# Two more gates in the stage of sums, keys at the opening of the memory heads, four begun products

## The chip, the cores and the metric

One core of a Trainium2 chip runs the whole kernel. The metric is the device time of one execution in microseconds (us), the median over runs.

The engines are PE (matmul; PEld is its weight load), DVE (vector), ACT (scalar), POOL (GpSimd) and SP, whose queue issues nearly all DMAs. Matmuls accumulate in banks of 128 x 512 float32 (PSUM), which ACT and DVE empty.

## What is computed

A two-layer encoder on 1024 tokens of width 1024, all in float32. The change lies in layer 2 (`l % 2 == 1`), in its front and its end:

```
h = rmsnorm(x, norm_gain[l])
mk, mv = jnp.split(memn @ w_mem_kv[l], 2, axis=-1)       # 256 memory tokens, 4 heads of 128
qc, kc, vc, qm, gate = split_cols(h @ w_in_odd[o], SPLIT_ODD)   # 1024, 1024, 1024, 512, 1536 columns
yc = neighborhood_attn(qc, kc, vc, rpb_c[o])             # 16 heads of 64 on a 16 x 64 grid, 8 x 16 windows
ym = memory_attn(qm, mk, mv)                             # 4 heads
y = jnp.concatenate([yc, ym], axis=-1) * jax.nn.silu(gate)
x = x + y @ w_out_odd[o]
return rmsnorm(x, final_norm_gain)
```

## The kernel before, in words

Every matmul operand of full precision is kept as two rounded parts, a high one and a low one (`wh`/`wl` for weights, `H` for the normalised tokens, `k`, `q`, `v`, `ph`/`pl` elsewhere); a product is the sum hi·hi + hi·lo + lo·hi, three matmuls for each 128 rows of the contraction. Columns of the projection come in tiles of 128: `O_Q` (8 tiles of queries), `O_K` (8 of keys, two heads each), `O_V` (8 of values), `O_QM` (4 memory queries), `O_G` (12 gates). A projected tile of 128 columns by 1024 tokens takes 48 matmuls of 512 columns.

Layer 2 has three stages.

*The stage of sums* (`front`, L1617). Pairs of column tiles are multiplied by seven products of half size instead of eight (sums and differences of token halves t1 to t4, of weight parts, and of results), 84 matmuls of 512 for a pair. `pairs` lists the pairs: eight gates (0 to 3 and 8 to 11), the memory queries and the queries; the tuple after it gives the order of the results' use, and `PLAN` says between which products the values of heads 0 to 3 are computed. Results go to HBM (`gd`, `mqd`, `qd`).

*The heads* (`odd`). First the eight half memory heads: `scores(n)` and the product with the memory values. Then the near heads (`near`), 16 heads over 136 steps, each with scores (`s`), the softmax (L1114 on DVE with its bias `bm`, L1117 on ACT or L1118/L1119 on DVE and POOL), a transpose of the result `pn` on PE (`tr`), the split into `ph` (ACT, L125) and `pl` (DVE, L542), and the product with the values (`pv`). A head's keys and values must be there when it starts. What layer 2 still has to project is the generator `work()`: its products are called *filler* and are put between the steps of the heads in a fixed ration of columns: 16 x 1536 columns ahead of the first score, `SLOT` columns at each of 32 places of the memory heads, `STEP` columns at each near step. In work() stand gate 4, the values of heads 4 to 7 (`of_two`, four blocks of 48 matmuls of 256 columns; a block fills one bank, and is then copied out by ACT L125 and DVE L425 in two halves), the keys (`keys(j)`, two halves of eight steps, 24 matmuls each; after the second half the high and low parts `k` are doubled to the other 64 partitions by DMAs, L366 and L367), gates 5, 6 and 7, and at last `begin_out`: the first two products of the output projection, which need the y rows 0 to 5 as operands (`first`, loaded at L1231 into tiles k, q and v, already in two parts). `todo` is the order of the later part; a task's weights are loaded while the one ahead of it runs.

PSUM has two banks each of the tags "s", "tr", "pv" and "pj". All filler goes through the two "pj" banks in turn.

*The output projection* (`out_project`, L1332 for products of y, L1345 for products of the sums t1 to t4 of y). It is again done by seven products. It takes the banks that `begin_out` has filled (`begun`), then adds its own. The sums t1 to t4 are split into high and low parts by ACT L125 and DVE L129, and results are added into `H`, `mk`, `sg`, `yb` tiles by DVE L1357.

PE runs its matmuls in the order of the program. The other engines' orders are set when the kernel is built, by a scheduler that weighs the instructions with offsets (`AHEAD`); each engine then runs its list in order, and so does SP's queue of DMAs.

## Time and profile before

| | |
|---|---|
| time, median of 3 runs | 1487.73 us (1485.93 to 1492.74) |
| profiled execution | span 1486.8 us; its own device time is not listed apart from the three runs, 1485.93, 1487.73 and 1492.74 us |
| PE busy | 1467.6 us, 99% |
| DVE, ACT, POOL busy | 1030.7, 837.2, 644.2 us |
| granted TensorE clock | 0.998 on average |
| memory heads | about 1030 to 1122 us |
| near heads | about 1123 to 1364 us |
| output projection | from 1364 us |

The profile's rows by time have the start, the length, the engine, the line, and out<-in by the names of the tiles; what stands in brackets is the idle time ahead and what ended it. A row of a chain is start, length and what ran or was waited for. A row of a table of windows has the window, its length, and for each engine its busy time with the number of instructions. A row of waits says who waited for whom: total, times, longest.

### The profile page before, as it was taken

The numbers are of one execution on the slowest core, as the hardware profiler recorded it, in microseconds if no ns is written. First come the engines' busy times: TensorE is split into PE (matmuls) and PEld (weight loads), VectorE is DVE, ScalarE is ACT, GpSimd is POOL, SyncE is SP. The second block draws the span as 40 slices with busy tenths as digits, with TensorE's granted clock in tenths as the row PEclk, the third lists the DMA queues.
The fourth block names the chain that finished last, engine by engine and source line by source line (L and its number), as shares of the span: only waits on it lengthen the run. The fifth ranks groups of instructions, "written<-read, shape, count | busy, mean of one in ns | idle before, by whom it ended". The sixth has DMA issues, their size and how long they took to land.

```text
span 1486.8 us, 25511 instructions
## 1 busy us (share of the span) xinstructions
PE 1467.6 (99%) x8433; PEld 1274.7 (86%) x8433; DVE 1030.7 (69%) x2124; ACT 837.2 (56%) x1877; POOL 644.2 (43%) x767
## 2 busy tenths in 40 slices
PE   9999999999999999999999999999999999999998
PEld 8898898988888788888879987888998898888886
DVE  6687777677776577776687776664446787778674
ACT  7743665556655456654544444444446777777454
POOL 1223668556765746543450000001425556665454
PEclk9999999999999999999999999999999999999999
DMA  8966334434443424388553343567665568789834
GB/s 287 306 160 181 118 125 160 123 120 133 126 137 112 155 78 144 100 276 303 187 176 127 128 135 137 157 169 241 233 242 170 188 198 269 246 283 323 314 105 144
DMA packets 173860, 271.92 MB, mean 183 GB/s; under 512 B 15648, under 2 KB 96800, under 8 KB 172704
## 3 DMA queue, kind: packets, MB, share of 16 engines
q1 hardware_dynamic: 173296, 270.20, 56.4%
q8 instruction: 67, 1.10, 0.3%
q14 instruction: 65, 0.53, 0.1%
q10 hardware_dynamic: 432, 0.09, 0.0%
HBM read 174.28 MB, written 83.89 MB: 174 GB/s over the span
## 4 chain that ended last, share of the span: by engine, by line
PE 86%; DMA 6%; DVE 3%; ACT 2%; issue 1%; SPq 1%; POOL 1%; POOLq 0%; ACTq 0%; DVEq 0%
PE pj L242 16%; PE pj L62 11%; PE x L1617 6%; PE tr L133 6%; PE pv L1066 4%; PE y L1617 4%; PE pv L62 3%; PE s L62 3%; PE pj L1332 3%; PE tr L62 3%; PE sa L1332 2%; PE pv L1617 2%; PE sa L1033 2%; PE s L1332 2%; PE sa L1034 2%; PE pj L851 2%
## 5 line engine op out<-in xcount | busy, mean ns | idle before, releaser
L542 DVE TENSOR_TENSOR pl<-tr,ph 128x512 fp32r<-128x512 f32 (+2 forms) x352 | 203.9, 594 | 45.5 <-ACT ph L125 43.6
L125 ACT ACTIVATE ph<-tr 128x512 fp32r<-128x512 f32 (+2 forms) x352 | 176.2, 522 | 103.7 <-PE tr L133 79.7
L242 PE MATMUL pj<-H,wh 128*128 128x512 f32 x704 | 233.2, 411 | 0.6 <-DVE vt L313 0.2
L158 POOL TENSOR_SCALAR wh<-wraw 128x512 fp32r<-128x512 f32 x48 | 32.2, 673 | 275.2 <-PE x L1617 236.0
L125 ACT ACTIVATE wh<-wraw 128x384 fp32r<-128x384 f32 (+1 forms) x163 | 88.7, 553 | 99.6 <-PE pj L1332 12.2
L242 PE MATMUL pj<-H,wl 128*128 128x512 f32 x352 | 139.2, 395 | 0.0
L242 PEld LDWEIGHTS pj<-H,wh 128*128 128x128 f32 x704 | 120.6, 189 | 19.3 <-issue 0.6
L62 PE MATMUL pj<-H,wh 128*128 128x512 f32 x384 | 121.0, 396 | 0.0
L1119 POOL TENSOR_SCALAR pn<-pn,st 128x384 f32<-128x384 f32 (+1 forms) x128 | 72.7, 569 | 102.1 <-DVE st L1118 62.0
L133 PE MATMUL tr<-ident,P 128*128 128x128 f32 x752 | 115.4, 273 | 0.3 <-POOL P L719 0.2
L1279 POOL TENSOR_TENSOR wl<-wraw,wh 128x384 fp32r<-128x384 f32 x56 | 62.9, 1125 | 91.5 <-ACT wh L125 89.2
L1117 ACT ACTIVATE pn<-pn,st 128x384 f32<-128x384 f32 (+1 forms) x128 | 75.1, 587 | 41.8 <-DVE st L1114 40.5
L133 PEld LDWEIGHTS tr<-ident,P 128*128 128x128 f32 x752 | 88.9, 140 | 8.2 <-POOL P L719 1.2
L1039 ACT ACTIVATE P<-sa,st 128x1024 f32<-128x1024 f32 x64 | 71.4, 1117 | 35.3 <-PE tr L133 19.1
L1041 POOL TENSOR_SCALAR P<-P,st 128x1024 f32<-128x1024 f32 x64 | 74.6, 1169 | 27.9 <-DVE st L1040 27.3
L1038 DVE TENSOR_REDUCE st<-sa 128x1 f32<-128x1024 f32 x64 | 77.5, 1218 | 8.3 <-PE sa L1034 7.6
L62 PE MATMUL s<-k,q 128*128 128x384 f32 (+1 forms) x352 | 81.2, 327 | 0.0
L242 PEld LDWEIGHTS pj<-H,wl 128*128 128x128 f32 x352 | 66.2, 188 | 15.1
L62 PE MATMUL pj<-H,wl 128*128 128x512 f32 x192 | 75.6, 394 | 0.0
L160 POOL TENSOR_TENSOR wl<-wraw,wh 128x512 fp32r<-128x512 f32 x52 | 69.6, 1341 | 10.3 <-ACT wh L125 7.8
L851 PE MATMUL pj<-ah,H 128*128 128x256 f32 x384 | 70.8, 282 | 1.0 <-ACT ah L125 0.6
L62 PEld LDWEIGHTS pj<-H,wh 128*128 128x128 f32 x384 | 66.6, 188 | 5.4
(568 smaller groups left out, 4186.7 us busy)
## 6 DMA issues: line engine op xcount, KB each, us to landing
wraw<-w_o SPq DMA_DIRECT2D x52, 256.0 KB, 3.7
y<-yb SPq DMA_DIRECT2D x24, 512.0 KB, 3.4
wraw<-s SPq DMA_DIRECT2D x64, 192.0 KB, 3.9
wraw<-w_e SPq DMA_DIRECT2D x44, 256.0 KB, 3.3
k<-k SPq DMA_DIRECT2D x42, 256.0 KB, 5.9
s<-bias SPq DMA_DIRECT2D x56, 192.0 KB, 2.0
wq<-w_o SPq DMA_DIRECT2D x40, 256.0 KB, 3.3
y<-sg SPq DMA_DIRECT2D x18, 512.0 KB, 3.5
```

The lines of the kernel that those rows point to most:

```text
L62: return lambda *a, **k: self.tc.keep_in_program_order(getattr(self.engine, name)(*a, **k))
L125: return self.nc.scalar.activation(out, in_, AF.Copy, scale=scale)
L133: self.turned = self.fence = self.pe.transpose(o, i, self.ident)
L242: self.pe.matmul(a[:, :n], s[:, kt % UNIT, :], m, start=(kt == 0 and i == 0), stop=(kt == KT - 1 and i == 2))
L542: self.low = nc.vector.tensor_tensor(pl[:, :n], tr[:, :n], ph[:, :n], op=OP.subtract)
L851: self.last = nc.tensor.matmul(a[:, b * 256:(b + 1) * 256], x[kt][:, t], w, start=(kt + b + i == 0), stop=(kt == KT - 1 and i == 2), skip_ ...
L1038: nc.vector.tensor_reduce(st[:, 0:1], s, axis=AX.X, op=OP.max, negate=True)
L1041: self.normal = nc.gpsimd.tensor_scalar(pt, pt, st[:, 2:3], 0.5, op0=OP.mult, op1=OP.mult)
L1117: nc.scalar.activation(o, o, AF.Exp, bias=st[:, 0:1], scale=-1.0, accum_out=st[:, 2:3])
L1119: self.normal = normal = nc.gpsimd.tensor_scalar(o, o, st[:, 3:4], 0.5, op0=OP.mult, op1=OP.mult)
L1332: last = nc.tensor.matmul(bank, s[:, k, :], y[3 * u + k][m][:, cols], start=start and u + k + e == 0, stop=u == 1 and k + e == 4, skip_gro ...
L1617: self.last = nc.tensor.matmul(bank, ws[s][:, k, :], b[k][m], start=start and k + i == 0, stop=k == UNIT - 1 and i == 2, skip_group_check= ...
```

## The change

Gates 4 and 5 leave the filler and become an eleventh pair of the stage of sums, run fourth. With less filler the rations change: 3400 columns a slot in the memory heads instead of 4150, and in the near heads 1825 for steps 0 to 108, 1125 for steps 109 to 119 and 2304 for steps 120 to 135, instead of 1930 for all.

The heads open with keys 0 instead of gate 4; both pairs of values (heads 4, 5 and 6, 7) use the tag "v" in one piece; seven steps of keys 1 come ahead of the second pair of values. Gate 7 goes through in two halves, the second at the very end.

`begin_out` makes four products instead of two, the last two in the banks of the tag "s"; the output projection starts with all four begun.

```
--- before.py
+++ after.py
@@ -24,8 +24,8 @@
 NEG = -1e30
 UNIT = 4
 PLAN = "x.xx.V1V1V2V1V1V1V2V1V1V1V2V1V1V1V2V1x2z2V1V1V2V1V1V1V2V1V1V1V2V1V1V1V2V1z4z2z2"
-SLOT = 4150
-STEP = 1930
+SLOT = 3400
+STEP = ((109, 1825), (120, 1125), (136, 2304))
 
 
 E_QA, E_KA, E_VA, E_QB, E_KB, E_VB, E_QM, E_G = 0, 4, 5, 6, 10, 11, 12, 16
@@ -1294,7 +1294,7 @@
         ws = deque(parts(0, u) for u in range(2))
         yield 0
         for i in range(n):
-            p = self.ps("pj")
+            p = self.ps("pj" if i < 2 else "s")
             banks.append(p)
             for u in range(2):
                 h, l = ws.popleft()
@@ -1302,7 +1302,7 @@
                     for e, (s, m) in enumerate(((h, 0), (h, 1), (l, 0))):
                         self.pe.matmul(p, s[:, k, :], first[3 * u + k][m], start=u + k + e == 0,
                                        stop=u == 1 and k + e == 4, skip_group_check=True)
-                    if k == 0:
+                    if k == 0 and i < 3:
                         ws.append(parts(i + 1, u))
                     yield 1536
         self.early = ws
@@ -1860,7 +1860,7 @@
                     if nt >= O_G:
                         return "gate", gd[nt - O_G]
                     return ("mem", mqd[nt - O_QM]) if nt >= O_QM else ("q", qd[nt])
-                pairs = [(n, n + 1) for n in (O_G + 8, O_G + 10, O_G, O_G + 2, O_QM, O_QM + 2, O_Q, O_Q + 2, O_Q + 4, O_Q + 6)]
+                pairs = [(n, n + 1) for n in (O_G + 8, O_G + 10, O_G, O_G + 2, O_QM, O_QM + 2, O_Q, O_Q + 2, O_Q + 4, O_Q + 6, O_G + 4)]
                 def values():
                     a, b = (self.values_of_two(wo[O_V + 2 * i:O_V + 2 * i + 2], vd[i], t, ("y", "pv"), "vt", 4, nc.vector)
                             for i, t in enumerate(("t3", "t4")))
@@ -1872,7 +1872,7 @@
                     yield from a
                     yield from b
                 v2 = values()
-                self.front(wo, pairs, (0, 1, 2, 4, 5, 6, 7, 8, 9, 3), v2, PLAN, x1, rows1, dests)
+                self.front(wo, pairs, (0, 1, 2, 10, 4, 5, 6, 7, 8, 9, 3), v2, PLAN, x1, rows1, dests)
             self.pools = {}
             mid.close()
             self.alias = {"P": "k"}
@@ -1903,9 +1903,8 @@
                         nc.sync.dma_start(io["out"][2 * p:2 * p + 2, :, c0:c0 + n].rearrange("k p t -> p k t"), x)
 
                 self.offset = AHEAD["out1"]
-                x = begun + [self.ps("s") for _ in range(2)]
                 y = [self.ps(t) for t in ("tr", "tr", "pv", "pv")]
-                self.out_project(io["w_oo"], sd[1], yd[1], x1d, done, OUT[1], (x, y), first, 2, last=True)
+                self.out_project(io["w_oo"], sd[1], yd[1], x1d, done, OUT[1], (begun, y), first, 4, last=True)
 
     def even(self, w, ka, qa, va, mq, qd, kvd, yd, sd, sd2):
         nc = self.nc
@@ -2017,28 +2016,26 @@
         half = lambda k, c: (O_G + k, self.gate_out(w, O_G + k, gd[k], [(c, 512)]))
 
         def work():
-            a, b = of_two(4, "v", 1), of_two(6, "k", 2)
-            g = self.gate_out(w, O_G + 4, gd[4])
-            now = next(g)
+            a, b = of_two(4, "v", 1), of_two(6, "v", 1)
+            k = keys(0)
+            now = next(k)
             next(a)
             yield now
-            yield from g
+            yield from k
+            self.ready[O_K + 1] = self.units(w, O_K + 1)
+            yield from a
+            made["bm"] = [self.near_bias(i) for i in range(2)]
             next(b)
-            yield from a
-            self.ready[O_K] = self.units(w, O_K)
+            k = keys(1)
+            for _ in range(7):
+                yield next(k)
             yield from b
-            k = keys(0)
-            now = next(k)
-            self.ready[O_K + 1] = self.units(w, O_K + 1)
-            yield now
-            yield from k
-            made["bm"] = [self.near_bias(i) for i in range(2)]
             made["v0"] = load_v(0)
-            todo = [(O_K + 1, keys(1)), (O_K + 2, keys(2)), half(5, 0), (O_K + 3, keys(3)), half(5, 512), (O_K + 4, keys(4)),
-                    (O_K + 5, keys(5)), half(6, 0), (O_K + 6, keys(6)), half(6, 512), (O_K + 7, keys(7)),
-                    (O_G + 7, self.gate_out(w, O_G + 7, gd[7]))]
+            made["open"] = True
+            todo = [(O_K + 1, k), (O_K + 2, keys(2)), half(6, 0), (O_K + 3, keys(3)), half(6, 512), (O_K + 4, keys(4)),
+                    (O_K + 5, keys(5)), half(7, 0), (O_K + 6, keys(6)), (O_K + 7, keys(7)), half(7, 512)]
             coming = iter(())
-            begin = self.begin_out(self.io["w_oo"], first, begun, 2)
+            begin = self.begin_out(self.io["w_oo"], first, begun, 4)
             for i, (_, steps) in enumerate(todo):
                 deque(coming, 0)
                 now = next(steps)
@@ -2046,8 +2043,6 @@
                     coming = self.jobs_of(w, todo[i + 1][0])
                 yield now
                 for k, now in enumerate(steps):
-                    if i == 0 and k == 6:
-                        made["open"] = True
                     if i == len(todo) - 1 and k == 4:
                         next(begin)
                     yield now
@@ -2115,7 +2110,7 @@
         while "open" not in made:
             fill(1)
         self.due = 0
-        self.near(made, load_q, load_v, gate, yd, lambda n: fill(STEP))
+        self.near(made, load_q, load_v, gate, yd, lambda n: fill(next(c for end, c in STEP if n < end)))
         deque(todo, 0)
         self.pe = nc.tensor
         return first, begun
```

On PE the values of heads 6, 7 look like this before: the last three matmuls of a block (`pj_2407`, the last block of heads 4, 5) and the first of the next one (`pj_2423`). The two are in different banks.

```order
L62 MATMUL pj_2407_11996<-v_2341_11571,H_1846_8875 128x256
L62 MATMUL pj_2407_11996<-v_2342_11572,H_1846_8875 128x256
L62 MATMUL pj_2407_11996<-v_2341_11571,H_1854_8883 128x256
L62 MATMUL pj_2423_12117<-k_2353_11658,H_1839_8868 128x256
L62 MATMUL pj_2423_12117<-k_2355_11660,H_1839_8868 128x256
L62 MATMUL pj_2423_12117<-k_2353_11658,H_1847_8876 128x256
```

And with the change, the end of the first block of heads 6, 7 (`pj_2485`) and the beginning of the second (`pj_2507`), with products of a memory head between them; both blocks are in the same bank, since the other is held by the first half of keys 1.

```order
L62 MATMUL pj_2485_12411<-v_2465_12323,H_1846_8875 128x256
L62 MATMUL pj_2485_12411<-v_2466_12324,H_1846_8875 128x256
L62 MATMUL pj_2485_12411<-v_2465_12323,H_1854_8883 128x256
L62 MATMUL pv_2494_12496<-ph_2497_12507,k_2440_12175 128x256 x2
L62 MATMUL pv_2494_12496<-pl_2498_12508,k_2440_12175 128x256
L62 MATMUL pv_2494_12496<-ph_2499_12511,k_2440_12175 128x256 x2
L62 MATMUL pv_2494_12496<-pl_2500_12512,k_2440_12175 128x256
L62 MATMUL pj_2507_12549<-v_2465_12323,H_1839_8868 128x256
L62 MATMUL pj_2507_12549<-v_2466_12324,H_1839_8868 128x256
L62 MATMUL pj_2507_12549<-v_2465_12323,H_1847_8876 128x256
```

What moved: two blocks in a row, in turn in two banks before, now use one bank, with six matmuls of 256 columns between them.

Key 6, whose doubled parts are read first by the score that begins its first head. Before, the last matmul of its second half (`pj_3195`) is followed by these rows on PE, and the first score that reads it (`k_3180` high, `k_3181` low) comes 79 rows later:

```order
L62 MATMUL pj_3195_15081<-H_1846_8875,wl_3098_14752 128x512
L62 MATMUL s_3240_15253<-k_3032_14523,q_3064_14625 128x384
L62 MATMUL s_3240_15253<-k_3033_14524,q_3064_14625 128x384
L62 MATMUL pv_3238_15238<-ph_3217_15167,v_3113_14802 128x384
L62 MATMUL pv_3238_15238<-pl_3218_15168,v_3113_14802 128x384
L62 MATMUL pj_3243_15264<-H_1839_8868,wh_3145_14919 128x512
```

```order
L62 MATMUL tr_3300_15450<-ident_1_63,pn_3257_15298 128x128
L62 MATMUL tr_3300_15450<-ident_1_63,pn_3260_15313 128x128
L62 MATMUL tr_3300_15450<-ident_1_63,pn_3269_15345 128x128
L62 MATMUL s_3303_15458<-k_3180_15042,q_3193_15075 128x256
L62 MATMUL s_3303_15458<-k_3181_15043,q_3193_15075 128x256
```

With the change, the last matmul of key 6 is on `pj_3246`, its parts are `k_3237` and `k_3238`, and only 28 matmuls stand between:

```order
L62 MATMUL pj_3246_15270<-H_1846_8875,wl_3146_14923 128x512
L62 MATMUL tr_3287_15435<-ident_1_63,pn_3254_15293 128x128
L62 MATMUL tr_3287_15435<-ident_1_63,pn_3260_15313 128x128
L62 MATMUL tr_3290_15442<-ident_1_63,pn_3254_15293 128x128
L62 MATMUL tr_3290_15442<-ident_1_63,pn_3260_15313 128x128
L62 MATMUL tr_3290_15442<-ident_1_63,pn_3269_15345 128x128
L62 MATMUL s_3293_15450<-k_3081_14698,q_3078_14689 128x384
L62 MATMUL s_3293_15450<-k_3082_14699,q_3078_14689 128x384
L62 MATMUL pv_3258_15304<-ph_3275_15380,v_3125_14853 128x384
L62 MATMUL pv_3258_15304<-pl_3276_15381,v_3125_14853 128x384
```

```order
L62 MATMUL tr_3308_15496<-ident_1_63,pn_3272_15362 128x128
L62 MATMUL tr_3311_15504<-ident_1_63,pn_3269_15345 128x128
L62 MATMUL tr_3311_15504<-ident_1_63,pn_3272_15362 128x128
L62 MATMUL tr_3311_15504<-ident_1_63,pn_3281_15394 128x128
L62 MATMUL s_3314_15512<-k_3237_15245,q_3208_15135 128x256
L62 MATMUL s_3314_15512<-k_3238_15246,q_3208_15135 128x256
```

What moved: the key's end, by the smaller ration of filler, towards the head that uses it. All 28 are of near steps and of the filler that follows (`pj_3296`, keys 7).

The end of the near heads on DVE, where the last low parts of the near heads (L542), the sums (L1357) and the low parts of t1 (`k_3596` and on, L129) follow each other. Before:

```order
L542 TENSOR_TENSOR pl_3564_16385<-tr_3562_16380,ph_3563_16384 128x384
L542 TENSOR_TENSOR pl_3567_16392<-tr_3565_16388,ph_3566_16391 128x256
L1357 TENSOR_TENSOR H_3576_16431<-H_3576_16431,pj_3492_16135 128x512
L1357 TENSOR_TENSOR H_3576_16431<-H_3576_16431,pj_3528_16265 128x512
L129 TENSOR_TENSOR k_3596_16507<-k_3596_16507 128x512
L129 TENSOR_TENSOR k_3597_16508<-k_3597_16508 128x512
L129 TENSOR_TENSOR k_3598_16509<-k_3598_16509 128x512
```

With the change, where the low parts of t1 are `k_3605` and on:

```order
L542 TENSOR_TENSOR pl_3581_16438<-tr_3579_16433,ph_3580_16437 128x384
L542 TENSOR_TENSOR pl_3584_16445<-tr_3582_16441,ph_3583_16444 128x256
L1357 TENSOR_TENSOR H_3591_16494<-H_3591_16494,pj_3477_16081 128x512
L1357 TENSOR_TENSOR H_3591_16494<-H_3591_16494,pj_3520_16220 128x512
L1357 TENSOR_TENSOR H_3592_16495<-H_3592_16495,s_3553_16337 128x512
L129 TENSOR_TENSOR k_3605_16522<-k_3605_16522 128x512
L129 TENSOR_TENSOR k_3606_16523<-k_3606_16523 128x512
L129 TENSOR_TENSOR k_3607_16524<-k_3607_16524 128x512
```

What moved: a third sum (`s_3553`, the third begun product) and a fourth low part now stand in this row, and on PE the products of t1 follow the near heads at once, where before the two products on `s_3570` and `s_3571` (36 matmuls of 512) came first.

49 lines of the change are left out of this document (22 added, 27 removed).

## Prediction

> **What bounds the kernel now.** I read the page first, then a table of stages, then the list of waits of layer 2, and last the single places that the change touches. The head of the page and its row of granted clock:
>
> ```profile
> span 1486.8 us, 25511 instructions
> PE 1467.6 (99%) x8433; PEld 1274.7 (86%) x8433; DVE 1030.7 (69%) x2124; ACT 837.2 (56%) x1877; POOL 644.2 (43%) x767
> PEclk9999999999999999999999999999999999999999
> ```
>
> The stages of layer 2 (front, memory heads, near heads in three pieces); the columns after the window are its length and the busy time of PE, PEld, DVE, ACT, POOL, then clock, DMA share and GB/s. Below it all that PE waited for from the memory heads to the end of the near heads:
>
> ```profile
> 920.00:960.00 40.00, 40.00 (x173) 32.20 (x172) 25.41 (x40) 17.60 (x30) 0.00 (x0) 1.00 0.57 175
> 1019.00:1100.00 81.00, 81.00 (x631) 78.50 (x630) 38.43 (x82) 38.41 (x113) 23.07 (x36) 1.00 0.67 231
> 1100.00:1300.00 200.00, 199.67 (x1176) 177.88 (x1175) 147.59 (x463) 139.50 (x367) 113.11 (x158) 1.00 0.71 226
> 1300.00:1345.00 45.00, 44.41 (x265) 39.45 (x264) 35.89 (x114) 33.48 (x90) 27.70 (x37) 1.00 0.83 293
> 1345.00:1364.00 19.00, 18.61 (x113) 16.12 (x113) 14.41 (x40) 13.40 (x34) 11.23 (x13) 1.00 0.91 327
> ...
> PE tr L62 <- DVE pl L542: 0.9, 2, 0.6
> PE pj L62 <- DMA v<-y: 0.2, 1, 0.2
> ```
>
> TensorE is the bound nearly everywhere, at full clock. In 345 us of layer 2's attention it stands still for 1.31 us (81 - 81.00, 200 - 199.67, 45 - 44.41, 19 - 18.61). So only two things move the time: fewer matmul columns, and waits that the new order opens on PE. The first can be counted; for the second I go, place by place, by the PE work that lies between an operand's last source and its use in the new order, set against the time that this path takes in the trace.
>
> The pace of PE, from the chain and, below it, from the list by time:
>
> ```profile
> 929.44 2.80 PE pv L1617 x12
> ...
> 949.04 2.80 PE pv L1617 x12
> ...
> 1364.32 8.40 PE s L1332 x36
> ...
> 1360.17 0.82 PE L62 MATMUL tr<-ident,pn 128*128 128x128 f32 x6
> 1360.74 0.42 PE L62 MATMUL pv<-ph,v 128*128 128x384 f32 x1
> ...
> 1363.28 0.34 PE L62 MATMUL pv<-pl,v 128*128 128x384 f32 x1
> 1363.46 0.34 PE L62 MATMUL pv<-ph,v 128*128 128x384 f32 x1
> ...
> 1363.89 0.28 PE L62 MATMUL pv<-ph,v 128*128 128x256 f32 x1
> 1364.01 0.32 PE L62 MATMUL pv<-pl,v 128*128 128x256 f32 x1
> ```
>
> A 512-column matmul is 2.80/12 = 8.40/36 = 0.233 us. A pair of gates in the stage of sums, with 84 of them, is 949.04 - 929.44 = 19.60 us without a gap. From start to start, 384 columns take 0.18, 256 columns 0.12 and 128 some 0.10 us; distances below are summed with these.
>
> **A. Two gates by seven products.** 2 x 48 = 96 matmuls leave, 84 come: -12 x 0.233 = **-2.8 us**. The front window has DVE at 25.4 and ACT at 17.6 of 40 us with DMA at 0.57: the added evictions (15 on DVE, 11 on ACT) and weight loads have room, so the new pair costs nothing beyond its products. The gates' stores and loads leave the memory heads; nothing waits for them there.
>
> **B. Values of heads 6, 7 with one bank.** In the new order the last values (four blocks of 48 products) come after seven of the eight steps of a key's first half. That half keeps one of the two "pj" banks until after the values, so all four blocks share the other, and each must wait until the block ahead is copied out. Before, blocks alternate, and the list of waits has no such wait. The way out of a bank, on PE, ACT and DVE:
>
> ```profile
> 1044.71 3.04 PE L62 MATMUL pj<-v,H 128*128 128x256 f32 x24
> ...
> 1046.35 0.38 ACT L125 ACTIVATE vt<-pj 128x256 fp32r<-128x256 f32 x1 [1.16 <-PE pj L62]
> ...
> 1046.77 0.42 DVE L425 TENSOR_TENSOR vt<-pj,vt 128x256 fp32r<-128x256 f32 x1 [1.12 <-ACT vt L125]
> 1047.64 0.43 DVE L425 TENSOR_TENSOR vt<-pj,vt 128x256 fp32r<-128x256 f32 x1 [0.45 <-ACT vt L125]
> ```
>
> Of the 24 products the first twelve end a block, at about 1044.71 + 12 x 0.12 = 1046.15; the other twelve begin the next block in the other bank at once. The bank is free at 1048.07: 1.92 us after its last product. In the new order six 256-column matmuls of a memory head stand between two blocks (0.7 to 0.85 us): 1.1 to 1.2 us of wait, three times. The fourth time it is the key's second half: there 1.7 us of near-head work lie between, but the block's second copy stands on DVE behind the first L1114 of the near heads, whose score ends just ahead of the waiting product; with L1114 (0.4), its accumulator read (0.1) and the copy (0.4) that is again about 1.1. Behind the waiting product PE has only its own order, and nothing overtakes: 3 x 1.2 + 1.1 = **+4.7 us**. Ends: 3 (each path 0.4 faster) and 7 (each 0.6 slower).
>
> **C. Keys that come later.** The filler columns per near step are changed, so each key ends elsewhere. Between key 6's last product and the first score that reads its low part the new order has 28 matmuls and one more, 9 x 0.233 + 4 x 0.176 + 5 x 0.12 + 11 x 0.105 = 4.55 us of PE work (before: 13.6). The path is copy on ACT, difference on DVE, then a DMA that doubles it to the other 64 partitions. Here for key 7, whose distance is the shortest before, with all landings of L367 in the last row:
>
> ```profile
> 1318.46 0.39 PE L62 MATMUL pj<-H,wl 128*128 128x512 f32 x1
> ...
> 1319.47 0.57 ACT L125 ACTIVATE k<-pj 64x512 fp32r<-64x512 f32 x1
> ...
> 1320.37 0.68 DVE L361 TENSOR_TENSOR k<-pj,k 64x512 fp32r<-64x512 f32 x1
> ...
> 1321.08 0.47 SPq L367 DMA_DIRECT2D k<-k  x1
> ...
> DMA to landing us min/median/max: 3.8/6.4/9.4
> ...
> k<-k SPq DMA_DIRECT2D x4, 256.0 KB, 5.8
> ...
> 1327.42 0.48 PE L62 MATMUL s<-k,q 128*128 128x256 f32 x2
> ```
>
> The row ahead of the last is key 7's four copies (5.8 median). From the product's end (1318.69) to the issue of L367 it is 2.4 us; with 5.8 to 6.4 until it lands, 8.2 to 8.8; I take 8.35. Key 6 then holds PE for 8.35 - 4.55 = **+3.8 us**. Ends: 2.4 + 3.8 - 4.55 = 1.7, and 2.4 + 9.4 - 4.55 = 7.2. Keys 4 and 7 have 8.0 us of work, as key 7 had: together **+0.3** (0 to 2).
>
> [...]
>
> **D. The begun products' operands.** Begin now makes four products inside the near heads, and the y rows 4 and 5 are loaded into the tile of near-head values ("v") when the last pair but one lets it go. In the new order 3.9 us of PE work lie between that release and the product with row 4 (5.9 for row 5); before, 9.6. SP's queue has nothing that waits longer ahead of it. L1231 issues these loads:
>
> ```profile
> 1344.37 0.93 SPq L1231 DMA_DIRECT2D v<-y  x2
> ...
> 1351.53 0.73 PE L62 MATMUL pj<-v,wh 128*128 128x512 f32 x2 [0.24 <-DMA v<-y]
> ...
> DMA to landing us min/median/max: 3.6/5.8/9.4
> ```
>
> The median 5.8 less 3.9 and 0.1 to issue: **+2.0 us** (0 with 3.6, 5.6 with 9.4); row 5 is then there.
>
> **E. From the near heads into the output projection.** Before, two products (8.40 us, L1332) lay between the last near product and the first one of t1 and hid its splits. They now run inside the last near steps, so their PE time is moved, not saved. What is late next is DVE:
>
> ```profile
> 1361.89 0.91 PE L62 MATMUL tr<-ident,pn 128*128 128x128 f32 x5
> 1362.55 0.48 PE L62 MATMUL pv<-ph,v 128*128 128x128 f32 x2
> ...
> 1363.00 0.89 DVE L542 TENSOR_TENSOR pl<-tr,ph 128x384 fp32r<-128x384 f32 x2 [0.70 <-ACT ph L125]
> 1363.80 1.27 DVE L1357 TENSOR_TENSOR H<-H,pj 128x512 f32<-128x512 f32 x2
> 1364.99 2.15 DVE L129 TENSOR_TENSOR k<-k 128x512 fp32r<-128x512 f32 x3
> ```
>
> From the last transpose (end 1362.55) to the last low part is 1.34 us; three sums (0.64 each) and one low part of t1 (0.72) follow: 4.0 us. The new order has 4.6 us of PE work there, because the fourth product is spread behind the last transpose. Some later rows (a weight's low part on POOL, a low part behind eight DVE instructions) come out within 0.5 us of their use: **+0.3 us** (0 to 2).
>
> **F. Old waits.** Of the 1.31 us above most hang on rows that are placed anew: **-0.8** (-1.3 to 0).
>
> **G. The thin steps.** Near steps 109 to 119 carry 1125 columns instead of 1930: each is 805 x 0.233/512 = 0.37 us shorter, with the same softmax work. DVE had 35.89 of 45 us in the row 1300 to 1345 with steps of about 1.8 us (25 scores in 45 us), 1.44 a step: all of the new 1.43 us, less the filler's own share, which shrinks with its columns. Three transposes and a score there come out with 1.25 to 1.75 us for a path of 1.34. I take **+0.6** (0 to 3.5: eleven steps of 0.3).
>
> Memory heads (3400 columns a slot) are shorter too, but DVE and ACT are at 38.4 of 81 us there, and no path but B's comes under what the trace shows. The order of loads in the front, the near bias, and the first values and keys at the opening keep their distances.
>
> **Sum.** -2.8 + 4.7 + 3.8 + 0.3 + 2.0 + 0.3 - 0.8 + 0.6 = +8.1 us, against a span of 1486.8. The median run, 1487.73, is 0.9 above that span; so 1487.7 + 8.1 = **1495.8 us**.
>
> **Rivals.**
> 1. Transfers land early. The memory heads and near heads lose two gates' stores and loads, so the queues are emptier than at 0.71 to 0.91. Key 6 at the 3.8 end and the y row at 3.6 take 2.1 and 2.0 off: 1491.7, within 0.5% of before. For it: the spread 3.8 to 9.4 within one kernel. Against: key 7's median of 5.8 stands in a stretch just like it. It decides already when key 6's copy lands in under 5.3 us.
> 2. DVE becomes the bound in the thin steps, at G's upper end: +2.9 more, 1498.7. For it: the 1.44 against 1.43. Against: part of it goes with the filler, and D's wait comes right behind these steps and makes up for DVE's delay.
> [...]
> 4. The waits don't show, since other work slips under them: -2.8 - 0.8: 1484.1. Against: PE has one order, and each wait has its distance.
>
> **Chances.** Forecast 0.48 (its own range 1492 to 1500), early transfers 0.25, DVE 0.15, cooling 0.05, no waits 0.07. A measurement of this kernel tells a change from none at about 0.5%: under 1480.3 or over 1495.2. Slower: 0.6 of the forecast, DVE and cooling, 0.49. Same: the rest of the forecast, early transfers and part of the fourth, 0.47. Faster is left with 0.04, as A and F together give 4.1. The range is 1487 to 1502: from most of the way to the fourth rival up to D's or C's upper end.
>
> **What would show it.** The page: PE's matmuls 12 fewer. The list of waits: PE on DVE L425 four times with about 1.1 us, PE on a "k" DMA for some 4 us about 70 us ahead of the near heads' end, PE on the "v" DMA for about 2. The opening of the output projection without a wait over 1 us. The near heads' windows: DVE above 90% in the thin stretch. Wrong would be: no waits on L425 (then the bank is not the limit), a key copy that lands within 4.6 us, or a wait over 3 us in the output projection.

## The result, and the profile after

The changed kernel takes 1513.5 us (median of 4 runs, 1511.1 to 1515.8) against 1489.2 (4 runs of the kernel before, 1485.9 to 1492.7): 1.0165 times as long, 95% interval 1.0147 to 1.0182. The direction was as forecast, slower; the size was not, +24 us instead of +8, and the time is outside the range. The profiled execution's own time is 1515.8 us, the longest of the four; its span is 1514.0, 27.2 above the span before.

The head of the page after:

```profile
span 1514.0 us, 25514 instructions
PE 1474.1 (97%) x8421; PEld 1277.3 (84%) x8421; DVE 1040.9 (69%) x2139; ACT 843.9 (56%) x1888; POOL 638.8 (42%) x759
```

Twelve matmuls fewer, as counted; PE is nevertheless busy 6.5 us longer. The table of windows over the same stretches as before (this kernel's stages lie about 20 us later); after the window: length, busy time of PE, PEld, DVE, ACT, POOL, clock, DMA share, GB/s:

```profile
1019.00:1100.00 81.00, 80.30 (x516) 72.27 (x515) 37.98 (x75) 35.88 (x95) 18.68 (x29) 1.00 0.74 229
1100.00:1300.00 200.00, 193.45 (x1227) 175.66 (x1227) 143.31 (x445) 136.06 (x365) 106.71 (x150) 1.00 0.65 210
1300.00:1345.00 45.00, 40.64 (x233) 36.31 (x232) 30.88 (x96) 29.51 (x77) 24.52 (x33) 0.92 0.75 227
1345.00:1364.00 19.00, 15.91 (x96) 13.59 (x95) 14.79 (x50) 13.66 (x38) 11.13 (x15) 1.00 1.04 350
```

Two things are new: PE stands idle in every stage of the heads (6.55 us of 200, 4.36 of 45, 3.09 of 19), and the granted clock, 1.00 in every window before, falls to 0.92 in one. The waits of PE in layer 2 (who waited for whom: total, times, longest):

```profile
PE s L62 <- DMA k<-k: 6.1, 4, 3.8
PE pj L62 <- DMA v<-y: 4.6, 1, 4.6
PE pj L62 <- DVE vt L425: 4.4, 4, 1.2
PE tr L62 <- DVE pl L542: 1.8, 2, 1.5
PE pj L1332 <- DVE wl L1279: 1.8, 1, 1.8
PE s L62 <- DVE st L1114: 1.7, 1, 1.7
```

The forecast had the first three rows, as 4.1, 2.0 and 4.7. The account can be closed by matmul: each one's start to the next start, less its pace (0.233, 0.176, 0.12, 0.105 us), summed over the stretches of each run.

| stretch, us | before | after | difference |
|---|---|---|---|
| 0 to 770 (ahead of all that is changed) | 18.7 | 20.3 | +1.5 |
| 770 to 1000 | 4.1 | 4.1 | 0.0 |
| 1000 to 1250 | 1.1 | 8.0 | +6.8 |
| 1250 to 1300 | 0.7 | 2.9 | +2.3 |
| 1300 to 1350 | 1.2 | 10.4 | +9.2 |
| 1350 to 1400 | 1.3 | 8.7 | +7.4 |
| from 1400 | 1.8 | 4.6 | +2.8 |

Together +30.0, less 12 products (2.8): the 27.2 between the spans. Of the 30.0, about 20 are the waits of the list; 5.4 are work at half clock (PE's busy time times one minus the clock, in steps of 1 us, summed from 1000 to 1480 us; "lost clock" below, nothing in the kernel before); 1.5 lies ahead of the change, where the programs are alike, and differs from run to run (17 to 22 us there in kernels below).

**The single waits**, from PE's list by time (start, length; in brackets the idle time ahead and what ended it):

```profile
1279.80 0.50 PE L62 MATMUL s<-k,q 128*128 128x256 f32 x2 [1.69 <-DVE st L1114]
...
1283.18 0.39 PE L62 MATMUL s<-k,q 128*128 128x256 f32 x1 [0.47 <-DMA k<-k]
...
1315.90 0.55 PE L62 MATMUL s<-k,q 128*128 128x256 f32 x1 [3.80 <-DMA k<-k]
...
1369.56 1.22 PE L62 MATMUL pj<-v,wh 128*128 128x512 f32 x2 [4.64 <-DMA v<-y]
```

Key 6's wait, 3.80, has the forecast's length, in part by luck: its low part was issued 1.6 us behind the key's last product (2.4 in the forecast) and landed 7.8 us later (5.8 to 6.4), and another 0.56 us of wait for it follows. The first two, around key 5, weren't forecast. SP's queue there (issue time, length, line), the transfers issued from 1264 to 1275 with their median time to landing, and DVE's row:

```profile
1265.11 0.38 SPq L1019 DMA_DIRECT2D v<-v  x1
...
1266.88 0.73 SPq L503 DMA_DIRECT2D y<-yb  x1
...
1269.43 0.47 SPq L366 DMA_DIRECT2D k<-k  x1
...
k<-k SPq DMA_DIRECT2D x4, 256.0 KB, 12.4
...
y<-yb SPq DMA_DIRECT2D x1, 256.0 KB, 11.6
...
1278.59 0.68 DVE L1158 TENSOR_TENSOR yb<-pv,bt 64x512 f32<-64x512 f32 x1 [3.29 <-issue]
```

Key 5's copies are now issued just behind the next head pair's loads (`v`, 1 MB, and others), and land 12.4 us after their issue; before, three of the four went out 3.1, 2.4 and 0.9 us ahead of that load and landed after 2.9 to 6.0 us (the fourth, 1.4 us behind it, took 9.1), in this row:

```profile
k<-k SPq DMA_DIRECT2D x4, 256.0 KB, 4.9
```

The store `y<-yb` is caught in the same crowd: 1266.88 + 11.6 = 1278.5. DVE's L1158 needs that `yb` buffer, starts at 1278.59, and with it the next L1114 and PE's score are late by 1.69 us. These two waits are the least stable of the list. In the kernels below that are edits of the changed one (all but the last), key 5's copies still go out behind the load of `v`, but the longest wait there is 0.82 us, and several have none; with the dummy work, with key 6 moved and half by half the copies land after 10.0 to 10.3 us (median) instead of 12.4. How much of the 1.69 belongs to the kernel, and how much to this one execution, stays open.

### The profile page after: what moved, and what is told of

The parts are those of the page before. It is cut to its first block, busy times and chain, and to the rows that moved or that the text cites. A ratio compares the mean times of both kernels' runs of the same rounds, so it can differ in the third digit from the quotient of the medians.

```text
span 1514.0 us, 25514 instructions
## 1 busy us (share of the span) xinstructions
PE 1474.1 (97%) x8421; PEld 1277.3 (84%) x8421; DVE 1040.9 (69%) x2139; ACT 843.9 (56%) x1888; POOL 638.8 (42%) x759
## 4 chain that ended last, share of the span: by engine, by line
PE 81%; DMA 7%; DVE 6%; ACT 2%; issue 2%; POOL 1%; SPq 1%; POOLq 0%; DVEq 0%; ACTq 0%
PE pj L242 15%; PE pj L62 10%; PE x L1617 7%; PE tr L133 5%; PE pv L1066 4%; PE y L1617 4%; PE s L62 4%; PE pv L62 3%; PE tr L62 3%; PE pj L1332 2%; PE sa L1332 2%; PE pv L1617 2%; DMA k<-k 2%; PE sa L1033 2%; PE sa L1034 2%
## 5 line engine op out<-in xcount | busy, mean ns | idle before, releaser
L542 DVE TENSOR_TENSOR pl<-tr,ph 128x512 fp32r<-128x512 f32 (+2 forms) x352 | 203.7, 594 | 58.1 <-ACT ph L125 56.3
L125 ACT ACTIVATE ph<-tr 128x512 fp32r<-128x512 f32 (+2 forms) x352 | 177.0, 523 | 109.7 <-PE tr L133 82.5
L242 PE MATMUL pj<-H,wh 128*128 128x512 f32 x704 | 233.3, 412 | 0.5 <-DVE vt L313 0.2
L125 ACT ACTIVATE wh<-wraw 128x384 fp32r<-128x384 f32 (+1 forms) x164 | 89.8, 553 | 106.0 <-PE pj L1332 14.1
L242 PE MATMUL pj<-H,wl 128*128 128x512 f32 x352 | 139.2, 395 | 0.0
L242 PEld LDWEIGHTS pj<-H,wh 128*128 128x128 f32 x704 | 120.5, 189 | 19.5 <-issue 0.6
L62 PE MATMUL pj<-H,wh 128*128 128x512 f32 x320 | 101.6, 399 | 1.0 <-DVE vt L425 1.0
L1279 POOL TENSOR_TENSOR wl<-wraw,wh 128x384 fp32r<-128x384 f32 x56 | 62.5, 1116 | 92.4 <-ACT wh L125 77.3
L125 ACT ACTIVATE wh<-wq 128x512 fp32r<-128x512 f32 x59 | 37.1, 630 | 69.5 <-PE x L1617 28.6
L1617 PE MATMUL x<-t,wh 128*128 128x512 f32 x232 | 73.2, 396 | 0.7 <-ACT wh L125 0.5
```

What stands on the lines that cost most here:

```text
L62: return lambda *a, **k: self.tc.keep_in_program_order(getattr(self.engine, name)(*a, **k))
L125: return self.nc.scalar.activation(out, in_, AF.Copy, scale=scale)
L242: self.pe.matmul(a[:, :n], s[:, kt % UNIT, :], m, start=(kt == 0 and i == 0), stop=(kt == KT - 1 and i == 2))
L542: self.low = nc.vector.tensor_tensor(pl[:, :n], tr[:, :n], ph[:, :n], op=OP.subtract)
L1617: self.last = nc.tensor.matmul(bank, ws[s][:, k, :], b[k][m], start=start and k + i == 0, stop=k == UNIT - 1 and i == 2, skip_group_check= ...
```

## The clock: a test stretch

Cooling of the clock has 0.05 among the chances. After's own windows show two, each beginning inside one of the two longest waits (the first is shown):

```profile
1310.98:1314.35 3.37, 1.12 (x8) 0.74 (x7) 2.44 (x6) 1.71 (x5) 1.97 (x4) 0.99 1.03 264
1314.40:1317.75 3.35, 1.29 (x4) 1.03 (x5) 0.03 (x1) 0.00 (x0) 0.00 (x0) 0.50 1.04 241
1317.75:1321.10 3.35, 3.35 (x11) 2.96 (x10) 1.13 (x5) 1.02 (x3) 1.73 (x2) 0.50 1.03 179
1321.10:1324.50 3.40, 3.40 (x22) 3.10 (x22) 2.05 (x6) 1.88 (x6) 1.18 (x2) 1.00 0.40 98
```

In the third row PE is busy all the time and gets through 11 matmuls, in the fourth through 22. It isn't a matter of this one execution: over the whole run the four executions of the changed kernel have a granted clock of 0.992 to 0.994, those of the kernel before, run beside the experiments, 0.996 to 0.999. To see what brings this on, and what decides a key copy's landing, a stretch was put behind the end of the kernel before:

```
+        mm = lambda n: [nc.tensor.matmul(p, d[:, :128], d[:, :512], start=True, stop=True) for _ in range(n)]
+        wait = lambda n: [nc.scalar.activation(d[:, :c], e[:, :c], AF.Copy) for c in n]
...
+            for n in WAITS[turn:] + WAITS[:turn]:
+                wait(n)
+                mm(41 + 3 * turn)
...
+            for work in 2, 4, 8:
+                for _ in range(3):
+                    wait(n)
+                    mm(work)
...
+                for i in range(n):
+                    nc.sync.dma_start(big[i], io["w_o"][4 * turn + 2 * i:4 * turn + 2 * i + 2].rearrange("k p c -> p k c"))
+                for i in range(2):
+                    nc.sync.dma_start(b[64 - 64 * i:128 - 64 * i, :].bitcast(F32), a[64 * i:64 * i + 64, :].bitcast(F32))
```

> The kernel before, with a test stretch behind its end that uses none of its results (its time is longer by some 600 us and is not compared). First part: bursts of 41 to 47 products of 512 columns (10 us), each behind a wait on ScalarE copies whose summed length goes from about 0.2 to 4 us, every length three times in another order. Theory A (what the changed kernel's trace suggests): the clock falls to 0.50 after some single waits of 2.5 us and after all above 3.5 us, and stays there for 3.5 to 6 us, never after one of 1.8 us or less. Theory B: only waits above 3.4 us do it; those of 2 to 3 us keep 1.00. Then three waits in a row of about 0.4, 0.9 and 1.3 us with 2, 4 or 8 products (0.5, 0.9, 1.9 us) between them: by A the longest three with 2 products between them bring the clock down although none is above 1.8 us; by B none does. Second part: two copies of 256 KB between partitions, issued right behind 0, 1, 2 or 3 loads of 1 MB on the same queue: if the landing time is set by what was issued ahead, 3 to 4 us with none and 2 to 3 us more for each MB, so 10 to 12 us behind 3 MB; if each transfer goes by its own bytes, 3 to 4 us in every case.

Measured. Single waits, by length, with how many of three were followed by a clock of 0.50: 0.41 to 1.65 us, none; 1.87, one; 2.08, three; 2.29, two; 2.95, one; 3.38 and 4.47, three. So neither theory: 2.08 us can do it, and 2.95 need not. What orders them is *when* they fall. All 33 changes of the clock in this stretch, down and up, lie on one grid of 3.4133 us, each within 0.01 us. Three windows of that grid and their successors (the busy time of PE, and ahead of the last three numbers of a row the other engines):

```profile
1570.75:1574.16 3.41, 1.89 (x8) 1.58 (x9) 0.00 (x0) 1.44 (x2) 0.00 (x0) 1.00 0.00 0
1574.16:1577.57 3.41, 3.41 (x16) 2.83 (x16) 0.00 (x0) 0.00 (x0) 0.00 (x0) 1.00 0.00 0
1581.00:1584.41 3.41, 1.33 (x6) 0.80 (x5) 0.00 (x0) 1.90 (x2) 0.00 (x0) 1.00 0.00 0
1584.41:1587.82 3.41, 3.41 (x10) 2.63 (x9) 0.00 (x0) 0.00 (x0) 0.00 (x0) 0.50 0.00 0
...
2089.59:2093.00 3.41, 1.31 (x5) 0.67 (x4) 0.00 (x0) 1.86 (x2) 0.00 (x0) 1.00 0.00 0
2093.00:2096.41 3.41, 3.10 (x7) 2.48 (x8) 0.00 (x0) 0.26 (x1) 0.00 (x0) 0.50 0.00 0
```

Of the windows of this stretch that ran at full clock, those in which PE was idle for 2.1 us or more were all followed by one at 0.50, those with up to 1.57 us by none; between, it went either way. The wait of 1.87 us in the first row is cut by the grid (1.52 inside), the 2.08 us of the third row lie in one window, and the last pair is two waits of 1.2 us with 4 products between them, which add up. Three waits of 0.78 us with 2 products between did it once, too. The half-clock spells here last one or two whole windows, 3.41 or 6.83 us, and PE gets through fewer products in them: 10 in the fourth row, where the second has 16, and 11 against 22 in the rows of the changed kernel above. The changes of clock in each kernel of this study lie on such a grid too, within 0.01 us. In the changed kernel the windows ahead of the two falls had 2.2 and 3.4 us of idle time, and the largest without one had 1.7. Up to the output projection one window does not fit: in the first of the two last kernels below, the clock falls at 1075.83 behind a window with 1.02 us of idle time. Six products in it start 1.61 us apart in all, where 0.72 is their pace; counted as idle, this makes 1.9. Whether the clock goes by the profile's busy time, no run shows. At that kernel's end it falls once more behind little idle time, 1.03 us (at 1488.84).

The second part: the scheduler put one copy of each pair ahead of the loads and one behind. A row `x2` joins a copy behind the loads with the next pair's first one; it starts with the former. SP's list and ScalarE's (the first read of the copied tile, and what it waited for):

```profile
2167.77 7.99 SPq L2233 DMA_DIRECT2D kb<-ka  x2
...
2177.16 10.07 SPq L2233 DMA_DIRECT2D kb<-ka  x2
...
2189.17 0.89 SPq L2233 DMA_DIRECT2D kb<-ka  x1
...
2165.95 0.31 ACT L2235 ACTIVATE d<-kb 128x128 fp32r<-128x128 f32 x1 [3.70 <-DMA kb<-ka]
2174.28 0.31 ACT L2235 ACTIVATE d<-kb 128x128 fp32r<-128x128 f32 x1 [7.09 <-DMA kb<-ka]
...
2185.41 0.31 ACT L2235 ACTIVATE d<-kb 128x128 fp32r<-128x128 f32 x1 [9.54 <-DMA kb<-ka]
...
2199.42 0.31 ACT L2235 ACTIVATE d<-kb 128x128 fp32r<-128x128 f32 x1 [12.09 <-DMA kb<-ka]
```

With nothing ahead a copy lands in 2.9 to 3.8 us; issued behind 1, 2 and 3 MB, in 6.5 (2174.28 - 2167.77), 8.3 and 10.3 us, and the same in the first turn. So in this stretch a copy's landing time depends on what was issued just ahead on its queue: it grows by 1.8 and 2.0 us with the second and third MB.

## Experiments on the changed kernel

Each is the changed kernel with one edit. Waits are those of PE's list.

**Dummy work ahead of the two longest waits.**

```
+            if n == 96:
+                for _ in range(20):
+                    self.pe.matmul(s[:, :384], qb, pair[5]["k"][1][0][:, 0:384], start=True, stop=True)
...
+                    if n == 4 and (i, u, k) == (0, 1, 1):
+                        spare.append(self.ps("pj"))
+                        for _ in range(16):
+                            self.pe.matmul(spare[0], h[:, 0, :], first[3][0], start=True, stop=True)
```

> The changed kernel with 36 matmuls more, whose results are overwritten: 20 of 384 columns (3.5 us) just ahead of the first score of key 6, where PE waits 3.8 us for the key's copy, and 16 of 512 columns (3.7 us) ahead of the product that waits 4.6 us for the v operand. Theory A (waits, and behind each long one some 5 us at half clock): PE no longer stands still for over 3.4 us, the clock stays at 1.00, and though PE has 7.2 us more to do the time falls by about 4.8 us against the changed kernel (1509 us). Theory B (only the waits cost time, the clock row is a by-product): the time stays at 1513 to 1514. Theory C (PE's work counts): up to 7 us more.

1510.2 us (1509.3 to 1510.7), span 1508.5: 36 more matmuls, 3.3 us less, near theory A's time. Both waits went, and with them the half clock behind them. But the wait for L542 grew to 3.4 us and cooled PE there, and the output projection's cluster of waits (0.7, 0.5, 1.8) cooled it too: lost clock 4.3 instead of 5.4. This does not yet show that idling costs more than its length: the dummy work takes 7.2 us in place of 9.0 us of waits (3.80, 0.56 and 4.64), and key 5's waits (2.2 us) are absent as well; together that is enough for the 3.3. What shows it are the rows at half clock above. That 3.4 us of standing still is where the clock begins to fall, as theory A has it, no run shows: in the test stretch it fell behind 2.08 us, three times of three.

**Key 6 ahead of gate 7's first half.**

```
-                    (O_K + 5, keys(5)), half(7, 0), (O_K + 6, keys(6)), (O_K + 7, keys(7)), half(7, 512)]
+                    (O_K + 5, keys(5)), (O_K + 6, keys(6)), half(7, 0), (O_K + 7, keys(7)), half(7, 512)]
```

> The changed kernel with the half of gate 7 that stands ahead of keys 6 put behind them: key 6 has 16.5 us of PE work to its first score instead of 4.4. Theory A: its wait (3.8 + 0.6 us) and the half clock behind it (about 2.1 us) go, 6.5 us less (1507). Rival (the DMA queues are full there, so a wait that goes at key 6 comes back at keys 5 and 7 or at the v operand): under 3 us less.

1505.1 us (1503.2 to 1506.5), span 1502.7, 8.4 less. Key 6's wait and the v wait are gone; new is one of 3.1 us for L1118 at 1337.8, and one for key 7 of 1.1; lost clock 4.1. That is theory A and a little more; key 5's waits, which the edit doesn't touch, are absent too.

**The first two begun products half by half**, so that the rows in `v` are needed 8.1 us later:

```
+        if n == 4:
+            order[1], order[2] = order[2], order[1]
```

> The changed kernel with the first two begun products taken half by half: rows 0 to 2 of both, then rows 3 to 5 of both, so that the v operand is needed 8.1 us of PE work after its tile is free instead of 3.9. Theory A: the wait of 4.6 us and the half clock behind it (about 2.7 us) go, 7 us less (1506.5). Rival (the stretch is bound by its transfers, and the wait moves to the next operand or into the output projection): under 3 us less.

1511.5 us (1509.8 to 1513.8), span 1508.4. The v wait is gone, and only 2.0 us with it (the ranges overlap): the wait for L542 is 2.5 us and key 6's 4.4, and the output projection cools too (lost clock 7.9). The rival held.

**A second bank for the values**: half of gate 6 instead of seven steps of key 1 ahead of the last values. In a first version its weights were loaded late.

```
+            yield from half(6, 0)[1]
+            yield from b
             k = keys(1)
-            for _ in range(7):
-                yield next(k)
-            yield from b
...
```

> The changed kernel with a half of gate 6 instead of seven steps of keys 1 ahead of the values of heads 6, 7 (and not later): no half key holds a bank through the values. Theory A: the four waits on L425 go (4.4 us in the list, about 5 with the pipeline's gaps), and key 6 comes 1.3 us earlier, so 5 to 8 us less (1506 to 1509). Rival (the copies out of the banks or the weights' splits bind there anyway): the waits stay under another name and less than 2 us is saved.

1524.9 us (1522.8 to 1526.2): the waits for L425 are gone, but PE waits 5.1 us for gate 6's weights; no answer. With the weights in time:

```
-            self.ready[O_K + 1] = self.units(w, O_K + 1)
+            self.ready[O_G + 6] = self.units(w, O_G + 6)
```

> As the kernel with half of gate 6 ahead of the values, but with that half's weights loaded ahead, as keys 1's were; keys 1's weights are loaded behind it. Theory A: no wait on L425 and none for the half's weights; key 6 has 5.9 us of PE work instead of 4.5. [...] Rival (the bank wait is only moved): 1511 to 1514.

1514.2 us (1509.9 to 1518.3), span 1512.5. The 4.4 us on L425 are gone, and nothing is won, as the rival has it. Its waits:

```profile
PE s L62 <- DMA k<-k: 9.2, 5, 4.1
PE pj L62 <- DMA v<-y: 5.0, 1, 5.0
```

What PE no longer waits for early, it waits for later here: 9.2 us for keys, 6.1 in the changed kernel, and 5.0 for `v`, against 4.6.

**All three together** (the last, key 6 moved, half by half):

> Three mends together: gate 6's half ahead of the values, gate 7's half behind keys 6, the first two begun products half by half. If the costs add up: -5 (banks), -8.4 (key 6, as measured), -2 to -7 (v operand): 1493 to 1498. Rival (all of them are one shortage of DVE and of the DMA queues near the end, which comes back elsewhere): above 1502.

1501.9 us (1499.6 to 1504.0), span 1497.9, between the theories. Left are 4.3 us around key 7, 1.9 and 1.4 in the output projection, and 5.6 of lost clock.

**Two begun products as before**, the ration spread over the rest:

```
-STEP = ((109, 1825), (120, 1125), (136, 2304))
+STEP = ((109, 1825), (136, 1141))
...
-            begin = self.begin_out(self.io["w_oo"], first, begun, 4)
+            begin = self.begin_out(self.io["w_oo"], first, begun, 2)
```

> The changed kernel with two begun products as before, the other two behind the near heads again, and 1141 columns a step from step 109 to the end. Theory A: the waits in the opening of the output projection (1.8 us and smaller ones) and most of the v operand's wait go, with the half clock behind it, about 8 us less; but 27 thin steps instead of 11 make PE wait for DVE, up to 4 more: 1505 to 1510. Rival (the output projection's waits come from DVE's arrears in the near heads, not from the missing cover): the waits on L1279 and L1357 stay, 1509 to 1513.

1509.5 us (1507.7 to 1509.8), span 1505.8. PE waits 7.7 us for keys, four times, and 4.4 on L425. The output projection has no wait and the excess from 1400 on is 1.9, as before (1.8; after 4.6); the v wait is 0.3 instead of 4.6, as theory A has it. Keys are worse, and so is the wait for L542 in the thin steps, 2.9 us in three; lost clock 6.0. Four begun products thus cost more than two, although the same matmuls are done.

**Four begun products alone**, in the kernel *before* (its ration 1945 up to step 119, then 2304; gates, values and keys as before):

> The kernel before with one part of the change alone: four begun products, in near steps 120 to 135 with 2304 columns, 1945 in the steps ahead. PE's work is the same, keys are not late, the v operand has 6.6 us. Theory A (the two products behind the near heads were cover for DVE): waits of 1.5 to 3 us in the output projection, perhaps half clock behind them (1.5), up to 2 at the v operand: 1491 to 1495. Rival (the step E as I priced it): 1489 to 1490.

1498.8 us (1496.2 to 1500.7, 5 runs), ratio 1.0068 (1.0043 to 1.0092), span 1497.0: 10 us slower. Theory A has the right places, but its time is 4 us short. All its larger waits, then ACT's list and DVE's ahead of the waits in the output projection:

```profile
PE pj L62 <- DMA v<-y: 2.5, 1, 2.5
PE pj L1332 <- DVE wl L1279: 2.4, 1, 2.4
PE pj L1332 <- ACT wh L125: 1.4, 1, 1.4
...
1401.92 0.63 ACT L125 ACTIVATE H<-H 128x512 fp32r<-128x512 f32 x1 [3.13 <-DMA H<-y]
...
1407.35 3.22 ACT L125 ACTIVATE H<-H 128x512 fp32r<-128x512 f32 x6
...
1408.00 0.69 DVE L129 TENSOR_TENSOR H<-H 128x512 fp32r<-128x512 f32 x1 [2.02 <-DMA wraw<-s]
...
1414.36 0.54 DVE L1279 TENSOR_TENSOR wl<-wraw,wh 128x384 fp32r<-128x384 f32 x1
```

The chain is: loads of y (`H<-y`) and of weight sums (`wraw<-s`), for which ACT waits 3.13 and 0.83 us; ACT's list, which then runs without a gap and comes to the next splits of `H` at 1407.35; and DVE's list, which can't go on before the first of these (done at 1407.97; the transfer that the row names had not wholly landed by then), runs without a gap from 1408.00, and has the weight's low part L1279 that PE needs at its end. The two products that the kernel before does behind the near heads (8.4 us) covered this chain: in that kernel, and in the one with two begun products as before, no wait stands there. Both idle spots cooled PE (2.4 us and 1.9 us of idle time in one window): lost clock 4.4. This is the cleanest case: 6.3 us of waits and 4.4 of half clock make the 10.

**Key 5's copies ahead of the load of v**:

```
-                if j < 7 and at == 8:
+                if j < 7 and at == 13:
                     pair["v"] = load_v(j + 1)
```

> Changed kernel with one edit: a near-head pair's values (1 MB) are loaded at the pair's 14th step instead of its 9th, so that key 5's copies are issued ahead of that load and not behind it. Theory A: the bytes issued just ahead set when a key copy lands: key 5's copies land in 4 to 7 us instead of 12.3, its waits of 1.7 + 0.5 us go, and the time falls by 2 us, to about 1511.5. Key 6's wait stays at 3 to 4 us. Rival: the queue is as full either way, the copies land in over 9 us, and the time stays within 1 us of 1513.5.

1514.2 us (1512.8 to 1519.1), span 1513.6. The edit doesn't change the order that it was meant to change. The load of `v` is issued, as in the changed kernel, 4.3 us ahead of the first of key 5's copies:

```profile
1264.28 0.38 SPq L1019 DMA_DIRECT2D v<-v  x1
...
1268.60 0.47 SPq L366 DMA_DIRECT2D k<-k  x1
...
k<-k SPq DMA_DIRECT2D x4, 256.0 KB, 8.5
```

So this run decides nothing between the theories. Both waits around key 5, 1.69 and 0.47, are gone and the copies land after 8.5 us instead of 12.4 (last row), but neither can be put down to the order. For theory A speaks the last kernel below, by its other ration: there a key's four copies go out 7.3 us ahead of this load and land after 5.9 to 6.9 us. The time didn't fall either: key 6's waits are 4.6 + 0.6, L542's 2.2, the v wait 3.4, and from 1000 us on four windows' ends bring the clock down instead of two: lost clock 8.3 against 5.4.

**Two attempts at a version that beats both**: the second bank, keys 4, 6 and 7 each ahead of a gate's half, v loaded at the 14th step, and two begun products half by half, with two rations:

```
+STEP = ((109, 1850), (136, 1040))        # the first
+STEP = ((100, 1880), (136, 1050))        # the second
```

> The gates in the stage of sums and keys at the opening are kept; everything that waited is mended: gate 6's half ahead of the values, keys 4, 6 and 7 ahead of the gate halves (12 us of PE work or more to their first scores), two begun products half by half with the other two behind the near heads, 1850 columns a near step to step 108 and 1040 from there. Theory A (12 products fewer and no new wait): PE work is 2.8 us less than before, so 1485 to 1489 against 1487.9, less what the 27 thin steps make PE wait for DVE (up to 3). Rival (less filler in the near heads costs more than the 12 products give, whatever the order): 1492 to 1498.

> The same with 1880 columns a near step to step 99 and 1050 from there: 36 thin steps, keys 2 to 6 up to 2 us earlier, key 7 later (9.4 us). If thin steps cost, 1 to 3 us more than the other; if late keys cost, less.

1495.7 us (1490.8 to 1498.6, 10 runs), ratio 1.0047 (1.0030 to 1.0064), and 1495.3 (1493.8 to 1498.8, 8 runs), 1.0048 (1.0034 to 1.0062). Some 18 of the 24 us come back, and both are still 7 slower than before; the two rations don't differ. The second one's excess is nearly that of before up to 1300 us, except for 3 us in its first 300, where nothing is changed: a spell at half clock from 224.5 us, behind a window with 2.0 us of idle time, where the changed kernel's window at this place has 1.5 and no spell. From 1300 to 1400 it is 10.6 instead of 2.5. There PE waits 2.4 us for key 7 in two pieces and 1.9 for DVE L1158, with two spells at half clock (lost clock 3.4). The last steps carry 1050 columns of filler instead of 1930. That they have too little of it to cover the same transfers fits all these runs, but no kernel here gave them more filler with all else kept, so it is an inference. Nothing tried beats the kernel before.

## Why the prediction was wrong, point by point

The direction and the places of B, C and D were right. What failed is the sum. It had no term for the half clock (5.4 us), put 0.3 us on what keys cost beside key 6's first wait (4.0) and 0.3 on what follows the near heads (2.8), and its D was less than half the wait (2.0 against 4.6).

- **A**, -2.8: right. 8433 to 8421 matmuls, and the stretch from 770 to 1000 has the same excess in both.
- **B**, 4.7: right, 4.4 in four waits of 1.0 to 1.2 us. As a price of the whole it is less: taken away (the second bank), nothing was won, though that edit also moves keys and loads.
- **C**: key 6, 3.8 forecast, 3.8 measured (and 0.6 more for the low part), with the two errors named above that nearly cancel. The step that failed is the +0.3 for the other keys: it looked at PE work between a key's last product and its use, and gave every copy one landing time. Key 5, which wasn't looked at, and key 7 got copies of 12.4 and 9.0 us (median), issued behind other loads: 0.5 and 1.3 us of wait, and 1.7 more through the store `y<-yb`, which holds up DVE. Rival 1, early transfers, erred the other way.
- **D**, 2.0: mis-sized, 4.6. It took 0.1 us from the release of `v` to the issue, since nothing ahead in SP's queue waits longer. But each issue waits there for the landing of an earlier transfer. The queue's issues, and below them a row of the list of its waits from 1355 to 1364:

```profile
1361.33 0.33 SPq L1291 DMA_DIRECT2D wraw<-w_oo  x1
...
1363.26 0.94 SPq L1231 DMA_DIRECT2D v<-y  x2
...
SPq L1231 <- DMA H<-x: 0.3, 1, 0.3
```

  In the trace SP's 959 DMAs use eight semaphores, and none is issued before the last one on its semaphore has landed: with each issue at most seven others are in flight. (Whether the queue itself could hold more, no run shows.) From 1355 to 1364 each issue starts 0.02 to 0.08 us behind a landing, with seven others in flight, and the loads of x and y land 0.64 to 0.66 us apart (1361.90 to 1364.50); the issue of `v` at 1363.26 follows a load of x that landed at 1363.20. With 6.3 us to land (1363.26 to 1369.5) and the forecast's 3.9 of PE work, the 4.6 leave 2.2 us between the release and the issue, three or four such places. That the wait hangs on when row 4 is needed is shown by the half-by-half edit, where it vanishes.
- **E**, 0.3: it looked at the wrong place. It counted DVE's work after the last transpose (4.0 us) against PE's (4.6), and took the DMAs for landed. The opening itself is as forecast, with no wait over 0.12 us. But some 35 us into the output projection, where L1332 takes up its next products, PE waits 1.8 us in the changed kernel and 3.8 in the kernel with four begun products alone, behind a chain of loads and the lists of ACT and DVE. The sum had no term for this place.
- **F**, -0.8: about right. The old waits on L542 (0.33 and 0.58) and on `v` (0.24) have gone, and one of 0.29 has come. A wait of 0.66 us for ACT L125 in the memory heads (1073.88) was in no term.
- **G**, 0.6: too small by 0.9 (the wait on L542 at 1347.6, 1.5), and wrong in manner: DVE was 30.9 of 45 us busy, less than before, and not the bound. Rival 2 falls.
- **Cooling**, half clock, has 0.05 among the chances and no term in the sum. It happened twice, at 6.8 us each, for 5.4 us. In the test stretch it went with the idle time in one window of 3.41 us, also in pieces. D's wait of 4.64 us puts at least half of it, 2.3 us, into one such window, wherever the grid cuts it; all windows of the stretch with that much cooled PE. Key 6's puts 1.9 us or more there, which did it in some: with waits of that length in the forecast, the term belonged in the sum. And the trace before has a place that shows it. At its very end PE waits 1.59 us, and the next window of the grid is at half clock, where it costs next to nothing, as hardly any product is left:

```profile
1477.46:1480.87 3.41, 1.82 (x17) 1.61 (x16) 2.41 (x9) 1.37 (x4) 1.94 (x2) 1.00 0.30 106
1480.87:1484.28 3.41, 0.09 (x1) 0.00 (x0) 1.79 (x3) 0.38 (x1) 1.27 (x2) 0.50 1.09 384
```

- **Rival 4**, waits that don't show: the opposite. Waits of 20 us took the place of a forecast of 11.7.

Between the spans it is 27.2 against a forecast of 8.1. Of the 19 us that were missing, 5.4 are the clock, 3.7 are keys 5 and 7, the held store and key 6's low part, 2.6 is D, 2.5 the output projection (2.8 more excess there, against 0.3), 0.9 is G, 0.7 the wait in the memory heads, and 1.5 the difference ahead of the change; B and F take some 0.5 off. The remaining 2 to 3 us are small waits that no run singles out.

What lies behind the change's loss is best seen from the removals. Edits that took away one or two waits gave back 3.3, 8.4, 2.0 and 0 us (dummy work, key 6, half by half, second bank): other waits grew in their place, and the clock fell in all four, behind windows of the grid with 1.9 to 3.4 us of idle time. The 22 us of gate products in the heads were work that TensorE had to do anyhow, and in the stage of sums they are 2.8 us cheaper. That in the heads they also covered transfers, and that this cover is what the heads now lack, fits the runs but is an inference; for the two products behind the near heads it is shown, by the kernel with four begun products alone.

## What to carry to other kernels

Where TensorE is at 99% and full clock, price a moved product twice: its own time, and what it covers where it stood; follow that cover through the transfers and the in-order lists, not only through the engines' work. Take a transfer's landing time from rows with the same bytes issued just ahead of it on its queue, not from the kernel's median (256 KB took 2.9 us in the test stretch with nothing ahead, 10.3 behind 3 MB), and its issue from the landings that the queue must wait for (it came 0.02 to 0.08 us behind one in the crowd from 1355 us on). And sum the idle time that the new waits put into any 3.4 us: in these traces windows with 1.6 us or more, and two with 1.0, were followed by one or two at half clock, though not every time (1.7 us in the changed kernel was not), and a spell ahead of a kernel's end cost 1.4 to 3.1 us.

## What was not expected of the hardware

In the test stretch all 33 changes of the clock lie on one grid of 3.4133 us. A full-clock window with 2.1 us or more of idle time was followed by one at 0.50 every time there, one with 1.57 or less never; elsewhere 1.59 was, once, at the end of the kernel before, and 1.02 and 1.03, by the profile's count, in the first of the two last kernels. So a wait of 2.08 us cooled PE three times out of three, and one of 2.95 us, cut by the grid, only once. It also differs where nothing is changed: some 220 us from the start, a window with 2.0 us of idle time had a spell behind it in the second of the last kernels, one with 1.5 had none in the changed kernel. 256 KB copied between partitions took from 2.9 us with nothing issued ahead to 12.4 us behind a head pair's loads. And in the changed kernel's trace none of SP's 959 DMAs was issued with more than seven others in flight; from 1355 to 1364 us, with seven, each issue came 0.02 to 0.08 us behind a landing.
